# Raw weight copies in the free buffers of the row sums and of the queries

## The chip, the cores and the metric

The kernel runs on one core of one Trainium2 chip. The metric is the device time of one execution in microseconds (us), given as the median of several runs. The core has five engines that work side by side, each through its own list in a fixed order: TensorE (PE) multiplies, VectorE (DVE) and ScalarE (ACT) work element by element, GpSimd (POOL) issues some transfers here, and SyncE (SP) issues most transfers from memory. An instruction that waits holds up everything behind it on its engine.

## What is computed

Two layers of a decoder trunk over 512 positions of width 1024. Each layer has three stages: a gated feed-forward block (`ffn1`), token mixing (`mix`), and a second feed-forward block (`ffn2`). Each stage begins with a norm whose shift, scale and gate are computed from a vector `c`.

```python
def swiglu(x, w_in, w_out):
    gate, up = jnp.split(x @ w_in, 2, axis=-1)
    return (jax.nn.silu(gate) * up) @ w_out
...
    for l in range(DEPTH):
        mod = (c_act @ w_ada[l] + b_ada[l]).reshape(B, N_MOD, D_MODEL)
        sh1, sc1, gt1, sh2, sc2, gt2, sh3, sc3, gt3 = [mod[:, i, None, :] for i in range(N_MOD)]
        hn = rms_norm(h, g_ffn1[l]) * (1.0 + sc1) + sh1
        h = h + 0.5 * (1.0 + gt1) * swiglu(hn, w_ffn1_in[l], w_ffn1_out[l])
        hn = rms_norm(h, g_mix[l]) * (1.0 + sc2) + sh2
        proj = hn @ w_mix_in[l]
        ...
        mixed = jnp.concatenate([y_att, y_rwkv, y_conv], axis=-1) @ w_mix_out[l]
        h = h + (1.0 + gt2) * mixed
        hn = rms_norm(h, g_ffn2[l]) * (1.0 + sc3) + sh3
        h = h + 0.5 * (1.0 + gt3) * swiglu(hn, w_ffn2_in[l], w_ffn2_out[l])
```

The inner width of the feed-forward blocks is 2816, that is 22 tiles of 128. The mixing joins sliding-window attention, a recurrent head group and a short convolution.

## The kernel before

The state `h` lies in memory on the chip as 8 tiles of 128 features by 512 positions. Weights come as tiles of up to 128 x 1024 (512 KB). Each product is made of three matmuls in a reduced format: a number is cast to its high part (`wH`, on ACT, line 101), the rest is its low part (`wL`, on DVE, line 102), and high x high, high x low and low x high are added up (`mm3`, lines 90 to 92). So a weight tile passes four steps: a transfer into a raw buffer `wraw` (`load_w`, line 267), the cast on ACT, the low half on DVE, and the matmuls. There are two `wraw` buffers and four of each half; a transfer waits until the low half of the tile before has read the buffer.

**A feed-forward stage** makes the gated activations in pairs of tiles. Most pairs go through `pair_in`, a scheme of seven products on halves of the matrices; it needs four sums and differences of the normed rows, P1, P2, T3 and T4, which lie in eight buffers with the tag `com` (a high and a low half of each, 4 KB a partition). In the last pair P1 is read in the first product, P2 and T3 later, T4 in the last product of all; after that the `com` buffers are free until the stage ends. Then the output: the 22 activation tiles are taken in two groups; for the second group, output tiles 0 to 5 (`pt`, loop over `i`) are made over all 512 positions, each followed on DVE by its residual (`residual`, line 309, `h <- ps_mm, cg, h`) and on ACT by a square for the next norm (`sq`, line 210), added to `ss` on DVE (line 206). Beside them run the columns that compute the next shifts, scales and gates (`wada`, line 163 on DVE, transfers by POOL).

**The end of a stage** is `close`, with tiles 6 and 7 in halves of 256 positions. PE runs the low half of tile 6, the low half of tile 7, then the high half of tile 6. After five steps of this it runs `stats` (`ps_ss`, line 229): small matmuls over `ss` and the squares of the two residual halves, then `rstd`, `spread` and `apply`, which make the normed rows `hnH`, `hnL` of the next stage while PE finishes tiles 6 and 7. In `close` DVE and ACT keep the order of the text. The halves of tile 7's weights have places of their own (`sum1`, `sum0`, `third`, `first`). The first four weight tiles of the next stage are loaded by the last element of `steps`, `ahead(k)`: 0 and 1 before `close` is called, 2 and 3 inside it. Outside of `close` a scheduler orders the instructions of each engine from the program order, dependencies and estimated costs; the last stage has no successor and its `ahead` does nothing.

**At the end of `mix`** the attention outputs stand in `qr` (the buffer of the queries, 8 KB a partition) until they are split to `y0` to `y3`. Weights of the output tiles come from `wmo1` and, for the last rows, `wmo2`; tiles 6 and 7 have 512 KB transfers. Beside this the recurrent part is finishing, with PE's products `ps_s` waiting for a copy `y` on ACT (line 951).

Of the kernel before, what the change touches and what calls it, by code (L numbers as in the profile page):

```python
# [8 lines left out]
F32 = mybir.dt.float32  # L9
F32R = mybir.dt.float32r  # L10
# [6 lines left out]
P = 128  # L17
# [3 lines left out]
KD = D // P  # L21
# [36 lines left out]
def trunk_kernel(ctx, tc, ins, out, layers=L, phases=("ffn1", "mix", "ffn2")):  # L58
# [24 lines left out]
    def psmm(tags=("mm",)):  # L83
        turn[0] += 1
        return psum([P, T], "ps_mm", tags[turn[0] % len(tags)])

    def mm3(acc, w, k, x, sl, start, stop):

        wH, wL, xH, xL = w[0][:, k], w[1][:, k], x[0][:, sl], x[1][:, sl]
        mm(acc, wH, xH, start=start, stop=False)  # L90
        mm(acc, wH, xL, start=False, stop=False)  # L91
        mm(acc, wL, xH, start=False, stop=stop)  # L92

    def mm6(acc, w, k, x, start, stop):

        for n, (a, b) in enumerate(((0, 0), (0, 1), (1, 0))):
            for sl in HALVES:
                mm(acc[:, sl], w[a][:, k], x[b][:, sl], start=start and n == 0 and sl is HALVES[0], stop=stop and n == 2, skip_group_check=True)  # L98

    def split(hi, lo, src):  # L100
        nc.scalar.copy(hi, src)  # L101
        nc.vector.tensor_sub(lo, src, hi.bitcast(F32))  # L102
# [15 lines left out]
    for i in range(KD):  # L118
        t = hp_.tile([P, T], F32, name=f"h{i}")
# [15 lines left out]
    for name, v in (("eps", EPS), ("eps64", 64 * EPS), ("gneps", GN_EPS), ("nhb", -HB)):  # L135
        t = const.tile([P, 1], F32, name=f"v_{name}")
# [53 lines left out]
    def ada_until(pool, crep, l, i):  # L190
        while todo and todo[0] <= (l, i, KD - 1):
            ada_steps(pool, crep, 1)


    def new_ss():
        return sp.tile([P, T], F32, name="ss", tag="ss")
# [66 lines left out]
    def load_w(src, n=KD, raw=None, pair=None):  # L263

        w = raw or wp.tile([P, KD, P], F32, name="wraw", tag="wraw", bufs=2)
        wH, wL = pair or (wp.tile([P, KD, P], F32R, name=x, tag=x, bufs=4) for x in ("wH", "wL"))
        loads.append(nc.sync.dma_start(w[:, :n], src))
        split(wH[:, :n], wL[:, :n], w[:, :n])
        return wH, wL
# [38 lines left out]
    def residual(pt, i, gate, ss, sl=ALL):  # L308
        done = stt(h[i][:, sl], pt, gate[:, i : i + 1], h[i][:, sl], ALU.mult, ALU.add)  # L309
        add_ss(ss, i, sl)  # L310
        return done

    def last_residual(pt, i, gate, ss, sl):

        residual(pt, i, gate, None, sl)
        return None if ss is None else square(i, sl)

    HAND = {mybir.EngineType.DVE, mybir.EngineType.Activation}

    def close(tiles, gate, ss, steps):  # L320

        stats, spread, apply, low, ahead = steps
        lo_, hi_ = HALVES

        def run(pt, seq, sl, first, at=()):
            for n, (w, k, x) in enumerate(seq):
                mm3(pt, w, k, x, sl, first and n == 0, n == len(seq) - 1)
                for m, f in at:
                    if m == n:
                        f()  # L330

        def half(i, pt, sl):
            return last_residual(pt, i, gate, ss, sl)

        def bank():
            return psmm(BANKS[1:3])[:, : T // 2]

        with tc.manual_schedule(engines=HAND):
            sqs = []
            for i, pt, rest, seq in tiles:  # L340
                first = pt is None
                pt = bank() if first else pt[:, : T // 2]
                run(pt, rest, lo_, first)
                sqs.append(half(i, pt, lo_))
            (i, _, _, seq), (i2, _, _, seq2) = tiles
            pt, late = bank(), []
            run(pt, seq, hi_, True, ((4, lambda: stats(lo_, sqs)), (7, lambda: spread(lo_))))
            ahead(2)
            apply(lo_, range(2))
            late.append(half(i, pt, hi_))  # L350
            apply(lo_, range(2, 4))
            pt = bank()
            run(pt, seq2, hi_, True)
            late.append(half(i2, pt, hi_))
            apply(lo_, range(4, 6))
            stats(hi_, late)
            apply(lo_, range(6, KD))
            spread(hi_)
            apply(hi_, range(4))
            ahead(3)  # L360
            apply(hi_, range(4, KD))
            return low()

    def ffn(l, w_in, w_pair, w_out, hn, im, ss, need, then, ready, first=None):
# [6 lines left out]
        with tc.tile_pool(name="act", bufs=1) as ap_:  # L371
            com = {n: tuple(ap_.tile([P, 4, H2], F32R, name=x, tag="com", bufs=8) for x in ("comH", "comL")) for n in ("P1", "P2", "T3", "T4")}
            ap_.tile([P, (512 - GAP) // 4], F32, name="gap", tag="gap")
            n_first = 2 if first is None else 4
            tiles = (t for t in projector([w_in[l, j, g] for j in range(2 * n_first) for g in range(2)], hn, BANKS[:3], first, 1, ready) if t is not None)
            xs, waiting, done, after = {}, [], [None], [None]
# [117 lines left out]
            def pieces(i, j0, j1, spare=False):  # L494
                n = (j1 - j0) // 2
                for k0 in (j0, j0 + n):
                    turn_[0] += spare
                    w = ap_.tile([P, KD, P], F32, name="wraw", tag="sum0", bufs=1) if spare and turn_[0] % 3 == 0 else None
                    yield k0, n, load_w(w_out[l, i, :, k0 : k0 + n], n, w)
# [5 lines left out]
            for g, (j0, j1) in enumerate(GROUPS):  # L505
# [26 lines left out]
                if g == 0:  # L532
                    cg = small_.tile([P, KD], F32, name="cg", tag="cg")
# [3 lines left out]
                for i in range(KD - 2 * g):  # L537
# [3 lines left out]
                    if g == 0:  # L541

                        k0, k1 = k1, KD if not todo or todo[0] > (l, im + 2, KD) else todo[0][2]
                        if k1 > k0:
                            ts(cg[:, k0:k1], mod[l, im + 2][:, k0:k1], -0.5, -0.5, ALU.mult, ALU.add)
                    pt = psmm(BANKS[:3])
# [2 lines left out]
                            mm3(pt, w, k, xs[k0_ + k], ALL, k0_ + k == j0, k0_ + k == j1 - 1)  # L549
                    done[0] = residual(pt, i, cg, ss if g else None)  # L550
            n = (j1 - j0) // 2
            seqs = [[(w, k, xs[k0 + k]) for k0, n_, w in list(pieces(KD - 2, j0, j1, True)) for k in range(n_)], []]
            for m, tags in enumerate((("sum1", "sum0"), ("third", "first"))):
                pair = tuple(ap_.tile([P, KD, P], F32R, name=x, tag=t, bufs=1) for x, t in zip(("wH", "wL"), tags))
                w = load_w(w_out[l, KD - 1, :, j0 + m * n : j0 + (m + 1) * n], n, None, pair)
                seqs[1] += [(w, k, xs[j0 + m * n + k]) for k in range(n)]
            ada_until(ap_, crep, *need)
            steps = then()
            for m in range(2):
                steps[-1](m)  # L560
            return close([(KD - 2 + m, None, seq, seq) for m, seq in enumerate(seqs)], cg, ss, steps)


    def mix(l, hn, ss, mp, then, ready):
# [5 lines left out]
        def pair(name):  # L570
            return rows_of(name != "y4", (name + "H", name + "L"))
# [32 lines left out]
        cm = small_.tile([P, KD], F32, name="cm", tag="cg")  # L604
# [4 lines left out]
        got = {}  # L609
# [483 lines left out]
        for q in range(2):  # L1093
            x = pair("yr")
            split(*x, yr[q])
            xr.append(x)
        steps = then()
        for n in range(2):
            w = load_w(wo2[l, n], 6)
            for d in range(3):  # L1100
                i = 3 * n + d
                pt = psmm(BANKS[1:3])
                for k in range(2):
                    mm6(pt, w, 2 * d + k, xr[k], k == 0, k == 1)
                residual(pt, i, cm, ss)
            steps[-1](n)
        xs = got["xs"] + xr
        seq = lambda w, ks: [(w, k, xs[k]) for k in ks]
        return close([(i, pt, seq(w, (6, 7)), seq(w, (4, 0, 1, 2, 3, 5, 6, 7))) for i, w, pt in got["last"]], cm, ss, steps)


    what = {"ffn1": ("g1", 0), "mix": ("gm", 3), "ffn2": ("g2", 6)}
    seq = [(l, p) for l in range(layers) for p in phases]

    def normed(n, ss):
        l, p = seq[n]
        g, im = what[p]
        return norm(l, g, im, im + 1, ss)
# [117 lines left out]
    with tc.tile_pool(name="first", bufs=1) as fp:  # L1236
        hn, first = begin(fp)
    ready = None
    for n, (l, p) in enumerate(seq):
        im = what[p][1]  # L1240
        nss = new_ss() if n + 1 < len(seq) else None
        nxt, ws = [], []

        def then():
            if nss is None:
                return [lambda *_: None] * 5
            nhn, scale, *steps = normed(n + 1, nss)
            nxt.append(nhn)
            scale()
            l2, p2 = seq[n + 1]  # L1250
            if p2 == "mix":
                srcs = [ins["wmi"][l2, k] for k in range(4)]
            else:
                srcs = [ins["w1i" if p2 == "ffn1" else "w2i"][l2, *divmod(k, 2)] for k in range(4)]
            return steps + [lambda k: ws.append(load_w(srcs[k]))]

        if p == "mix":
            with tc.tile_pool(name="mix", bufs=1) as mp:
                marks = mix(l, hn, nss, mp, then, ready)
        else:  # L1260
            w, need = ("w1", (l, 7)) if p == "ffn1" else ("w2", (l + 1, 1))
            marks = ffn(l, ins[w + "i"], ins[w + "p"], ins[w + "o"], hn, im, nss, need, then, ready, first)
        first = None
        hn, ready = (nxt[0], (ws, marks)) if nxt else (None, None)
# [85 lines left out]
```

## Time and profile before

| what | value |
|---|---|
| median of 3 runs | 1927.6 us (1924.51 to 1929.95) |
| the profiled execution | 1933.48 us, span 1931.1 us |
| mean granted clock of PE | 0.993 |
| busy: PE, DVE, ACT, POOL | 98%, 73%, 44%, 7% of the span |
| moved by transfers | 308.46 MB, mean 160 GB/s |

A line of the timeline has the start in us, the duration, the engine, the source line, the operation, result and operands, the shape, and in brackets the idle time before it with what ended it. A line of the stretches has the stretch, its length, the busy time of PE, PE's weight loads, DVE, ACT and POOL (with the number of instructions), then the granted clock of PE, the busy share of the transfer engines, and GB/s. A line of the waits has who waited and for what, the total in us, how often, and the longest. The profiled execution is one run with the profiler on, so its time is compared with its own rows, and only differences are carried over to the median.

### The profile page before, as it was taken

Reading aid. Unit: us, or ns where it says so; the run is one execution under the profiler, and the core shown is the slowest. Engines: PE = TensorE matmul, PEld = TensorE weight load, DVE = VectorE, ACT = ScalarE, POOL = GpSimd, SP = SyncE. Lnnn points to the kernel's source line nnn. Section 1 sums busy time; section 2 is a strip of 40 time slices with the busy share of each in tenths; the row PEclk is TensorE's granted clock in tenths of the full one; section 3 lists DMA queues with packets and bytes.
Section 4 is the critical chain, followed back from the end, with each engine's and each line's share of the span. In section 5 each row is a group of like instructions: output and inputs, shape, how many; then the busy total and the mean of one; then the engine's idle time right before and its main releaser. Section 6 shows DMA issues by size and latency. Waiting matters only on the chain. (4 is left out here: it accounts for less than half of the span.)

```text
span 1931.1 us, 37043 instructions
## 1 busy us (share of the span) xinstructions
PE 1887.2 (98%) x15504; PEld 1748.1 (91%) x15504; DVE 1401.1 (73%) x2181; ACT 838.7 (43%) x1264; POOL 130.8 (7%) x212
## 2 busy tenths in 40 slices
PE   8999999999999999999999999999999999999999
PEld 7998899897889999899899988989878899998998
DVE  6687687758976777677878767786598667773862
ACT  4443255346322554155345514534562234532551
POOL 0101100100000000110100021010000000110000
PEclk8999999999999999999999999999999999999999
DMA  7767875621312476886647687662321215764742
GB/s 297 250 162 228 256 197 171 213 77 45 79 39 83 121 197 174 282 211 173 227 127 193 168 274 218 183 224 95 92 61 49 70 51 167 192 216 133 186 124 86
DMA packets 104326, 308.46 MB, mean 160 GB/s; under 512 B 23392, under 2 KB 24416, under 8 KB 103136
## 3 DMA queue, kind: packets, MB, share of 16 engines
q1 hardware_dynamic: 75936, 203.33, 32.2%
q0 software_dynamic: 28224, 102.77, 21.3%
q8 instruction: 121, 1.98, 0.4%
q14 instruction: 45, 0.37, 0.1%
HBM read 302.66 MB, written 3.41 MB: 158 GB/s over the span
## 5 line engine op out<-in xcount | busy, mean ns | idle before, releaser
L101 ACT CAST wH<-wraw 128x1024 fp32r<-128x1024 f32 (+2 forms) x292 | 268.8, 922 | 533.2 <-PE ps_mm L91 176.3
L102 DVE TENSOR_TENSOR wL<-wraw,wH 128x1024 fp32r<-128x1024 f32 (+2 forms) x292 | 308.8, 1059 | 126.4 <-ACT wH L101 125.0
L90 PE MATMUL ps_mm<-actH,wH 128*128 128x512 f32 (+1 forms) x784 | 289.1, 369 | 0.0
L92 PE MATMUL ps_mm<-actH,wL 128*128 128x512 f32 (+1 forms) x784 | 288.7, 368 | 0.0
L91 PE MATMUL ps_mm<-actL,wH 128*128 128x512 f32 (+1 forms) x784 | 288.6, 368 | 0.0
L441 PE MATMUL ps_d<-comH,wH 128*128 128x256 f32 x816 | 228.3, 280 | 4.5 <-ACT s L463 3.9
L442 PE MATMUL ps_d<-comL,wH 128*128 128x256 f32 x816 | 226.9, 278 | 0.0
L443 PE MATMUL ps_d<-comH,wL 128*128 128x256 f32 x816 | 226.9, 278 | 0.0
L98 PE MATMUL ps_mm<-hnH,wH 128*128 128x256 f32 x1040 | 214.7, 287 | 5.0 <-ACT hnH L101 2.9
L98 PE MATMUL ps_mm<-hnL,wH 128*128 128x256 f32 x1040 | 212.5, 283 | 0.0
L98 PE MATMUL ps_mm<-hnH,wL 128*128 128x256 f32 x1040 | 209.9, 282 | 0.5 <-DVE wL L102 0.5
L163 DVE SCALAR_TENSOR_TENSOR wada<-wada,crep 128x1024 f32<-128x1024 f32 x140 | 167.7, 1220 | 47.3 <-DMA wada<-in_wadaT 46.9
L102 DVE TENSOR_TENSOR wL<-sum,wH 128x1024 fp32r<-128x1024 f32 x102 | 124.9, 1225 | 71.1 <-ACT wH L101 70.8
L98 PEld LDWEIGHTS ps_mm<-hnH,wH 128*128 128x128 f32 x1040 | 160.3, 190 | 16.0 <-issue 8.2
L101 ACT CAST wH<-sum 128x1024 fp32r<-128x1024 f32 x102 | 107.5, 1054 | 149.3 <-PE ps_d L442 70.0
L92 PEld LDWEIGHTS ps_mm<-actH,wL 128*128 128x128 f32 x784 | 148.3, 189 | 24.5 <-DVE wL L102 0.3
L91 PEld LDWEIGHTS ps_mm<-actL,wH 128*128 128x128 f32 x784 | 148.3, 189 | 24.4
L90 PEld LDWEIGHTS ps_mm<-actH,wH 128*128 128x128 f32 x784 | 148.4, 189 | 24.2
L98 PEld LDWEIGHTS ps_mm<-hnL,wH 128*128 128x128 f32 x1040 | 160.9, 190 | 6.7 <-issue 5.7
L98 PEld LDWEIGHTS ps_mm<-hnH,wL 128*128 128x128 f32 x1040 | 160.4, 191 | 4.0 <-issue 2.9
L441 PEld LDWEIGHTS ps_d<-comH,wH 128*128 128x128 f32 x816 | 154.7, 190 | 7.1 <-ACT s L463 5.1
L442 PEld LDWEIGHTS ps_d<-comL,wH 128*128 128x128 f32 x816 | 154.6, 190 | 0.0
(402 smaller groups left out, 4240.9 us busy)
## 6 DMA issues: line engine op xcount, KB each, us to landing
wada<-in_wadaT POOLq DMA_DIRECT2D x128, 512.0 KB, 4.8
wraw<-in_wmi SPq DMA_DIRECT2D x40, 512.0 KB
wraw<-in_w2p SPq DMA_DIRECT2D x36, 512.0 KB
wraw<-in_w1p SPq DMA_DIRECT2D x32, 512.0 KB
wraw<-in_w1o SPq DMA_DIRECT2D x32, 384.0 KB
wraw<-in_w2o SPq DMA_DIRECT2D x32, 384.0 KB
wraw<-in_w1i SPq DMA_DIRECT2D x20, 512.0 KB
wraw<-in_w1o SPq DMA_DIRECT2D x32, 320.0 KB
```

Source lines behind the costliest of these rows:

```text
L90: mm(acc, wH, xH, start=start, stop=False)
L91: mm(acc, wH, xL, start=False, stop=False)
L92: mm(acc, wL, xH, start=False, stop=stop)
L98: mm(acc[:, sl], w[a][:, k], x[b][:, sl], start=start and n == 0 and sl is HALVES[0], stop=stop and n == 2, skip_group_check=True)
L101: nc.scalar.copy(hi, src)
L102: nc.vector.tensor_sub(lo, src, hi.bitcast(F32))
L163: stt(w, w, 1.0, crep, ALU.mult, ALU.mult, accum_out=out_)
L441: mm(pt[:, i], wH, x[k][0], start=start and i + k == 0, stop=False, skip_group_check=True)
L442: mm(pt[:, i], wH, x[k][1], start=False, stop=False, skip_group_check=True)
L443: mm(pt[:, i], wL, x[k][0], start=False, stop=k == 3, skip_group_check=True)
```

## The change

The raw copies get other places. In a feed-forward stage eight raw tiles take the tag `com`: two for output tile 6, two for tile 7, and four for the next stage's first weights. In `mix` the next stage's first two raw tiles take the buffer of the queries; the other two stay in `wraw`.

```diff
@@ close
-    def close(tiles, gate, ss, steps):
+    def close(tiles, gate, ss, steps, raws):
...
-            ahead(2)
+            ahead(2, raws[0])
...
-            ahead(3)
+            ahead(3, raws[1])
@@ ffn, after the output tiles 0 to 5
-            seqs = [[(w, k, xs[k0 + k]) for k0, n_, w in list(pieces(KD - 2, j0, j1, True)) for k in range(n_)], []]
-            for m, tags in enumerate((("sum1", "sum0"), ("third", "first"))):
-                pair = tuple(ap_.tile([P, KD, P], F32R, name=x, tag=t, bufs=1) for x, t in zip(("wH", "wL"), tags))
-                w = load_w(w_out[l, KD - 1, :, j0 + m * n : j0 + (m + 1) * n], n, None, pair)
-                seqs[1] += [(w, k, xs[j0 + m * n + k]) for k in range(n)]
+            raws = [ap_.tile([P, KD, P], F32, name="wraw", tag="com", bufs=8) for _ in range(8)]
+            seqs, own = [], (("sum1", "sum0"), ("third", "first"))
+            for i in (KD - 2, KD - 1):
+                seq = []
+                for m in range(2):
+                    pair = None if i < KD - 1 else tuple(ap_.tile([P, KD, P], F32R, name=x, tag=t, bufs=1) for x, t in zip(("wH", "wL"), own[m]))
+                    k0 = j0 + m * n
+                    w = load_w(w_out[l, i, :, k0 : k0 + n], n, raws.pop(0), pair)
+                    seq += [(w, k, xs[k0 + k]) for k in range(n)]
+                seqs.append(seq)
...
             for m in range(2):
-                steps[-1](m)
+                steps[-1](m, raws.pop(0))
@@ mix
         steps = then()
+        raws = mp.tile([P, 2, KD, P], F32, name="wraw", tag="qr")
...
-            steps[-1](n)
+            steps[-1](n, raws[:, n])
@@ then
-            return steps + [lambda k: ws.append(load_w(srcs[k]))]
+            return steps + [lambda k, raw: ws.append(load_w(srcs[k], KD, raw))]
```

PE's and POOL's lists keep their order. DVE's list at the end of the first feed-forward stage (640 columns: a half of an output tile's weights, 1024: a weight tile of the next stage; h_96, h_98 and h_100 are the residuals of tiles 5, 6 and 7), before:

```order
L309 SCALAR_TENSOR_TENSOR h_96<-ps_mm,cg,h_96 128x512
L102 TENSOR_TENSOR wL<-wraw,wH 128x640
L206 TENSOR_TENSOR ss<-ss,sq 128x512
L102 TENSOR_TENSOR wL<-wraw,wH 128x1024
L309 SCALAR_TENSOR_TENSOR h_98<-ps_mm,cg,h_98 128x256
L102 TENSOR_TENSOR wL<-wraw,wH 128x1024
L309 SCALAR_TENSOR_TENSOR h_100<-ps_mm,cg,h_100 128x256
L232 RECIPROCAL rstd<-rstd 128x2
```

The same place on DVE with the change:

```order
L102 TENSOR_TENSOR wL<-wraw,wH 128x1024
L309 SCALAR_TENSOR_TENSOR h_96<-ps_mm,cg,h_96 128x512
L102 TENSOR_TENSOR wL<-wraw,wH 128x1024
L206 TENSOR_TENSOR ss<-ss,sq 128x512
L220 SCALAR_TENSOR_TENSOR gmod<-mod_7_3657,par 128x8
L309 SCALAR_TENSOR_TENSOR h_98<-ps_mm,cg,h_98 128x256
L309 SCALAR_TENSOR_TENSOR h_100<-ps_mm,cg,h_100 128x256
L232 RECIPROCAL rstd<-rstd 128x2
```

Both 1024-column halves now stand ahead of the residual of tile 6, and the residuals of tiles 6 and 7 follow each other.

SP's list at the same stage's end with the change (3820 to 3823 are the raw tiles of output tiles 6 and 7, 3824 to 3827 those of the next stage; the others belong to output tiles 1 and 2):

```order
L267 DMA wraw_3822<-in_w1o 128x640
L267 DMA wraw_3823<-in_w1o 128x640
L267 DMA wraw_3548<-in_w1o 128x640
L267 DMA wraw_3569<-in_w1o 128x640
L267 DMA wraw_3824<-in_wmi 128x1024
L267 DMA wraw_3825<-in_wmi 128x1024
L267 DMA wraw_3605<-in_w1o 128x640
L267 DMA wraw_3626<-in_w1o 128x640
L267 DMA wraw_3826<-in_wmi 128x1024
L267 DMA wraw_3827<-in_wmi 128x1024
```

Before, all sixteen rows from `in_w1o` stood ahead of the first from `in_wmi`; now the loads into `com` stand between those of the output tiles, two by two as the products free their places.

SP's list at the end of the first `mix` (6934 and 6941 are the weights of output tiles 6 and 7), before and with the change:

```order
L267 DMA wraw_6879<-in_wmo1 128x768
L267 DMA wraw_6934<-in_wmo1 128x1024
L267 DMA wraw_6941<-in_wmo1 128x1024
L267 DMA wraw_7011<-in_wmo2 128x768
L267 DMA wraw_7066<-in_w2i 128x1024
```

```order
L267 DMA wraw_6879<-in_wmo1 128x768
L267 DMA wraw_7011<-in_w2i 128x1024 x2
L267 DMA wraw_6934<-in_wmo1 128x1024
L267 DMA wraw_6941<-in_wmo1 128x1024
L267 DMA wraw_7012<-in_wmo2 128x768
```

The next stage's first two loads moved from behind the `wmo1` rows to ahead of 6934. DVE and ACT keep their order at this place.

More of the change, by code (lines that the diff above doesn't have):

```diff
@@ L559, in ffn @@
             for m in range(2):
-                steps[-1](m)
-            return close([(KD - 2 + m, None, seq, seq) for m, seq in enumerate(seqs)], cg, ss, steps)
+                steps[-1](m, raws.pop(0))
+            return close([(KD - 2 + m, None, seq, seq) for m, seq in enumerate(seqs)], cg, ss, steps, raws)
     def mix(l, hn, ss, mp, then, ready):
@@ L1105, in mix @@
                 residual(pt, i, cm, ss)
-            steps[-1](n)
+            steps[-1](n, raws[:, n])
         xs = got["xs"] + xr
         seq = lambda w, ks: [(w, k, xs[k]) for k in ks]
-        return close([(i, pt, seq(w, (6, 7)), seq(w, (4, 0, 1, 2, 3, 5, 6, 7))) for i, w, pt in got["last"]], cm, ss, steps)
+        return close([(i, pt, seq(w, (6, 7)), seq(w, (4, 0, 1, 2, 3, 5, 6, 7))) for i, w, pt in got["last"]], cm, ss, steps, (None, None))
     what = {"ffn1": ("g1", 0), "mix": ("gm", 3), "ffn2": ("g2", 6)}
```

## The prediction

> **What bounds the kernel now.** I read the page first: the busy shares, then the engine TensorE (PE) alone through its waits, then two-microsecond stretches of the span, and last the instructions in time order around the stretches with a hole.
>
> ```profile
> span 1931.1 us, 37043 instructions
> PE 1887.2 (98%) x15504; PEld 1748.1 (91%) x15504; DVE 1401.1 (73%) x2181; ACT 838.7 (43%) x1264; POOL 130.8 (7%) x212
> PE ps_ss L229 <- ACT sq L210: 4.6, 3, 1.8
> PE ps_s L956 <- ACT y L951: 3.7, 2, 2.5
> ```
>
> The page's second line and two lines of PE's waits. PE is busy for 98% of the span, so 1931.1 - 1887.2 = 43.9 us is all that can be won while it does the same work, and the change leaves PE's own list of instructions as it was. The longest wait in total is `ps_ss <- sq`: 4.6 us, three times, the longest 1.8. It stands in `close`, once after each feed-forward stage that has a successor. Three stretches show them:
>
> ```profile
> core 0: us, PE busy (x) PEld busy (x) DVE busy (x) ACT busy (x) POOL busy (x), PEclk, DMA share, GB/s
> 374.00:376.00 2.00, 0.57 (x6) 0.48 (x5) 1.62 (x2) 0.25 (x2) 0.00 (x0) 1.00 0.38 152
> 376.00:378.00 2.00, 1.63 (x14) 1.64 (x15) 0.17 (x1) 0.80 (x3) 0.00 (x0) 1.00 0.78 199
> 972.00:974.00 2.00, 0.97 (x11) 0.89 (x9) 1.18 (x2) 0.42 (x1) 0.00 (x0) 1.00 0.22 72
> 1320.00:1322.00 2.00, 0.70 (x8) 0.61 (x6) 1.62 (x2) 0.26 (x1) 0.00 (x0) 1.00 0.55 207
> 1322.00:1324.00 2.00, 1.52 (x13) 1.53 (x14) 0.08 (x1) 0.79 (x3) 0.00 (x0) 1.00 0.65 188
> 1324.00:1326.00 2.00, 2.00 (x13) 2.00 (x13) 1.23 (x3) 0.82 (x1) 0.00 (x0) 0.61 0.19 78
> 1326.00:1328.00 2.00, 2.00 (x12) 2.00 (x12) 1.81 (x6) 0.91 (x2) 0.00 (x0) 0.53 0.39 106
> 1328.00:1330.00 2.00, 2.00 (x20) 2.00 (x19) 1.50 (x4) 1.35 (x3) 0.00 (x0) 1.00 0.40 156
> ```
>
> PE lacks 1.43 + 0.37 = 1.8 us at 374 to 378, 1.03 at 972 and 1.30 + 0.48 = 1.78 at 1320. The two rows after that last hole show something more: the granted clock is 0.61 and 0.53, and 25 matmuls pass in 4 us where the next row has 20 in 2. Why PE waits is seen on the engines ahead of it (VectorE is DVE, ScalarE is ACT), in time order:
>
> ```profile
> 367.79 0.73 ACT L101 CAST wH<-wraw 128x640 fp32r<-128x640 f32 x1 [3.48 <-DMA wraw<-in_w1o]
> 373.10 1.05 ACT L101 CAST wH<-wraw 128x1024 fp32r<-128x1024 f32 x1 [0.41 <-DMA wraw<-in_wmi]
> 374.18 1.23 DVE L102 TENSOR_TENSOR wL<-wraw,wH 128x1024 fp32r<-128x1024 f32 x1 [1.94 <-ACT wH L101]
> 375.32 0.48 DVE L309 SCALAR_TENSOR_TENSOR h<-ps_mm,cg,h 128x256 f32<-128x256 f32 x1
> 375.90 0.42 ACT L210 ACTIVATE sq<-h 128x256 f32<-128x256 f32 x1 [1.75 <-DVE h L309]
> ...
> 372.27 0.28 PE L90 MATMUL ps_mm<-actH,wH 128*128 128x256 f32 x1
> ...
> 374.07 0.28 PE L229 MATMUL ps_ss<-ones_r,ss 128*128 128x1 f32 x2
> ...
> 376.37 0.38 PE L229 MATMUL ps_ss<-ones_r,sq 128*128 128x1 f32 x2 [1.80 <-ACT sq L210]
> ```
>
> The residual of output tile 7 (375.32) had its sum ready at about 372.3, when PE began the next run. It stands in DVE's row behind the low half of the next stage's second weight tile, which waits for ACT's cast, which waits for a transfer into one of two `wraw` buffers. The chain is transfer, cast, low half, residual, square, statistic: a transfer ends last.
>
> **The change part by part.** *1. The loads at the end of a feed-forward stage.* The four transfers of tiles 6 and 7 (320 KB each) and four of the next stage (512 KB each) are free of the two `wraw` buffers; their places come free with the products P1, P2, T3 and T4 of the last pair. On DVE the next weights now stand ahead of tile 5's residual, so the residuals of tiles 6 and 7 follow each other. I follow the first stage. The last gating column of this stage ends on DVE at 364.05:
>
> ```profile
> 362.90 1.23 DVE L163 SCALAR_TENSOR_TENSOR wada<-wada,crep 128x1024 f32<-128x1024 f32 x1
> 369.29 0.69 DVE L206 TENSOR_TENSOR ss<-ss,sq 128x512 f32<-128x512 f32 x1
> 365.68 0.74 DVE L309 SCALAR_TENSOR_TENSOR h<-ps_mm,cg,h 128x512 f32<-128x512 f32 x1
> ```
>
> Behind it come three low halves of 640 columns, two of 1024, tile 5's residual and its addition to `ss`, and tile 6's residual. With the pitches of these rows that is 3 x 0.8 + 2 x 1.2 + 0.7 + 0.7 + 0.4 = 6.6 us: DVE is free for tile 7 at about 370.6, and PE ends that half at 372.3. So tile 7's residual runs 372.4 to 372.9 and its square to 373.4, before PE reaches the statistic at 374.07. There is 0.7 us in hand on this path and 1.7 on DVE. The term is -(1.8 + 1.0 + 1.8) = -4.6 us; its ends are 0, if all three statistics are as late as before, and -4.6, since a wait cannot fall below zero. I take -4.6, since the chain clears it. After the statistic nothing moves against PE: `rstd`, `ahead(2)` and the norm stand in the same row as before.
>
> *2. The half clock.* Besides the one at 1324 there are three more such stretches, all after holes that the change leaves:
>
> ```profile
> 690.00:692.00 2.00, 2.00 (x11) 2.00 (x11) 0.00 (x0) 0.00 (x0) 0.00 (x0) 0.50 1.01 328
> 1538.00:1540.00 2.00, 0.85 (x8) 0.66 (x6) 0.61 (x1) 1.05 (x1) 0.00 (x0) 1.00 0.10 40
> 1540.00:1542.00 2.00, 0.59 (x6) 0.53 (x7) 1.93 (x4) 1.02 (x3) 0.00 (x0) 1.00 0.29 33
> 1544.00:1546.00 2.00, 2.00 (x12) 1.88 (x10) 0.28 (x1) 0.00 (x0) 0.00 (x0) 0.50 0.67 197
> 1640.00:1642.00 2.00, 2.00 (x12) 2.00 (x11) 0.00 (x0) 0.00 (x0) 0.00 (x0) 0.53 0.97 383
> ```
>
> One costs 4 us less the 2.7 that 25 matmuls need at 37 to 38 in 4 us: 1.3 us. Of the three removed holes one was followed by it, so I take -1.3; the ends are 0 and two of them, -2.6, as both 1.8 us holes are alike.
>
> The Trainium skill ("TensorE: Matmul & The Clock Gate", Part 1, "What's actually happening") says that the clock halves after an idle window of about 3.4 us of a free-running counter and asks for no idle gap longer than that. By this rule a hole of 1.8 us would halve nothing, and the sum would be -4.6 alone. The trace differs: 1.8 us of idle at 1320 was followed by 4 us at 0.57. The same page's free-running window would explain why the equal hole at 374 was not.
>
> *3. Early transfers beside the last pair and the output tiles.* SP issues in order, so tiles 1, 2 and 3 of the output weights now stand behind transfers that wait for PE. DMA has room there, and little later:
>
> ```profile
> 304.00:308.00 4.00, 4.00 (x37) 4.00 (x37) 4.00 (x5) 2.18 (x4) 0.00 (x0) 1.00 0.29 112
> ...
> 320.00:324.00 4.00, 4.00 (x38) 4.00 (x37) 2.58 (x4) 1.50 (x3) 0.00 (x0) 1.00 0.37 109
> 324.00:328.00 4.00, 4.00 (x21) 3.36 (x20) 3.49 (x5) 3.25 (x6) 0.00 (x0) 1.00 0.41 103
> 340.00:360.00 20.00, 20.00 (x90) 16.57 (x89) 17.52 (x32) 5.98 (x9) 4.22 (x8) 1.00 0.92 303
> 318.91 0.73 ACT L101 CAST wH<-wraw 128x640 fp32r<-128x640 f32 x1 [1.19 <-PE ps_d L442]
> ...
> 327.97 0.71 ACT L101 CAST wH<-wraw 128x640 fp32r<-128x640 f32 x1
> ```
>
> T3's product ends near 319 (it released the cast at 318.91), T4's near 325, where PE changes to the output tiles (21 matmuls in 4 us for 38). Behind the two 512 KB transfers that T3 frees, 1 MB at the 303 GB/s of the third row is 3.5 us, so tile 2's weights land by about 325, ahead of their cast at 327.97. I cost this at 0. Its cover is that cast's lead over PE: at 90 matmuls in 20 us a tile of 30 takes 6.7 us, so tile 2 is multiplied from about 338. In the busy stretch 340 to 360 there is now less to move.
>
> *4. The end of the mixing stage.* Two 512 KB loads into the queries' buffer stand on SP ahead of the weights of output tiles 6 and 7 and start when the last query is split, at 575.3.
>
> ```profile
> 574.63 0.68 DVE L102 TENSOR_TENSOR y3L<-qr,y3H 128x512 fp32r<-128x512 f32 x1
> 576.00:580.00 4.00, 4.00 (x71) 3.70 (x70) 1.62 (x2) 1.43 (x2) 0.00 (x0) 1.00 0.00 0
> 583.31 1.78 ACT L101 CAST wH<-wraw 128x1024 fp32r<-128x1024 f32 x2 [4.65 <-DMA wraw<-in_wmo]
> 596.44 1.05 ACT L101 CAST wH<-wraw 128x1024 fp32r<-128x1024 f32 x1 [3.10 <-PE ps_mm L98]
> ```
>
> They fall into 576 to 580, when DMA is idle. 1 MB takes 3.5 us, until about 579.7, which is when tile 6's load can start (its buffer is read out then). The gain is nothing, since the cast they serve (596.44) waits for PE. The price is 0; its ends are 0 and +1 us in each of two layers, were half of one transfer still in the way. I take 0 by the row that shows no traffic.
>
> *5. The last stage* has no successor. There ACT and DVE each get one split of tile 7 ahead of `up` in the last pair.
>
> ```profile
> 1866.64 0.69 DVE L478 TENSOR_TENSOR up<-ps_d,up 128x512 f32<-128x512 f32 x1 [1.25 <-PE ps_d L443]
> ```
>
> With 0.7 us more on ACT and 0.8 on DVE `up` moves to at most 1868.1, and PE needs its bank only after another product of 24 matmuls, 2.6 us, at about 1869.1. I take 0, with ends 0 and +0.5. The four small constants of `mix` move to a later place on DVE, of 0.1 us each in rows that PE does not wait for: 0.
>
> **Sum.** -4.6 - 1.3 = -5.9 us. Against the profiled execution's 1933.48 us this gives 1927.6. That execution lies 5.9 us above the median of three runs, 1927.6, to which I apply the same difference: 1921.7 us.
>
> **The rivals.**
> (a) The holes close and the clock gains nothing, because in most executions no half-clock stretch followed them, or because another hole catches it: 1927.6 - 4.6 = 1923.0. For it: the hole at 374 had none. Against: the one at 1320 had.
> (b) Something is late next. If the gating columns end 3 us later than 364, DVE reaches tile 7 at 373.6 and a good half of each hole stays: about 1925. For it: DMA at 0.92 of its time at 340 to 360. Against: the change takes traffic out of that stretch.
> (c) Slower: at the mixing end tile 6's weights come late behind the two early loads, and cast, low half, tile 7's load and the `ps_s` wait (2.5 us already at 1538) all shift. It decides from 3 us in each of the two layers, which cancels 5.9; at 4 us it gives about 1930. For it: the casts there already wait 4.65 us for such a load. Against: the idle row at 576.
> (d) The statistic is as late as before, for a reason other than DVE's row: 1927.6. Against: DVE's order itself changes there.
>
> **How the numbers follow.** Forecast 0.52, (a) 0.20, (b) 0.13, (c) 0.08, (d) 0.07. About 0.3%, 5.8 us, is what a measurement of this kernel tells from no change, so the line lies at 1921.8, on the forecast itself. The forecast's own range is 1919 to 1924, as none to two half-clock stretches are saved; six tenths of it (0.31) lie beyond the line, and I add half of (a) for runs in which the old kernel met more of them: faster 0.41, slower 0.08 from (c), same the rest, 0.51. The range runs from 1917, where the two stretches and a spread of the runs (1924.51 at the lowest, 3 us below the median) come together, to 1927.5, which takes in (a), (b) and half of (d).
>
> **What would show it.** Right: PE's waits have no `ps_ss <- sq` over 0.3 us; the two half-tile residuals (L309, 128x256) no longer have a 1024-column low half between them; no half clock after the three places; the first transfers of `in_wmi` start before 330. The `ps_s <- y` wait stays at 2 to 4 us in total: if it has grown to 7, (c) is true. Wrong: new waits of PE for `wH` or `wL` among the output tiles, or `ps_d` waiting for `up` in the last pair.

## The result, and the profile after

| | before | changed | ratio, 95% interval |
|---|---|---|---|
| median, first comparison | 1928.57 us (10 runs) | 1921.68 us (10 runs) | 0.9963 [0.9951, 0.9976] |
| median, the changed kernel run again | 1929.63 us (20 runs) | 1919.63 us (5 runs) | 0.9945 [0.9932, 0.9958] |
| profiled execution | 1933.48 us, span 1931.1 | 1922.28 us, span 1920.5 | |

The changed kernel is faster by 6.9 us in the first comparison and by 10.0 us in the second. The forecast was 5.9 us. Both intervals lie below 1. Two of the first lines of the page after:

```profile
span 1920.5 us, 37038 instructions
PE 1884.7 (98%) x15504; PEld 1747.4 (91%) x15504; DVE 1400.5 (73%) x2181; ACT 838.1 (44%) x1264; POOL 130.9 (7%) x212
```

The four longest of PE's waits (who waited for what, total us, times, longest):

```profile
PE ps_g L443 <- DVE wL L102: 4.5, 3, 2.6
PE ps_d L441 <- ACT s L463: 3.6, 2, 1.8
PE ps_s L961 <- ACT y L956: 3.1, 2, 2.0
PE ps_mm L98 <- ACT hnH L101: 2.9, 1, 2.9
```

`ps_ss <- sq`, 4.6 us and first in the list before, is no longer in it. Lines 956 and 961 are 951 and 956 of before; the change added five lines above them. The three places now lie at 370, 962 and 1310. The stretches there, columns as before (PE, PEld, DVE, ACT, POOL busy with counts, then the granted clock, the transfers' share and GB/s):

```profile
370.00:372.00 2.00, 2.00 (x19) 2.00 (x18) 0.64 (x2) 0.84 (x2) 0.00 (x0) 1.00 0.00 0
372.00:374.00 2.00, 2.00 (x20) 2.00 (x19) 0.05 (x1) 0.35 (x2) 0.00 (x0) 1.00 0.00 0
...
964.00:966.00 2.00, 2.00 (x19) 2.00 (x18) 0.48 (x1) 0.42 (x1) 0.00 (x0) 1.00 0.00 0
...
1312.00:1314.00 2.00, 2.00 (x20) 2.00 (x18) 0.48 (x1) 0.42 (x1) 0.00 (x0) 1.00 0.04 8
1314.00:1316.00 2.00, 2.00 (x19) 2.00 (x19) 0.17 (x1) 0.71 (x2) 0.00 (x0) 1.00 0.00 0
```

PE is busy in all of each, at full clock, and almost nothing is transferred: the weights had come earlier, their transfers issued on SP from 317 on (two rows of SP in time order, the duration being that of issuing):

```profile
316.99 0.80 SPq L267 DMA_DIRECT2D wraw<-in_wmi  x2
...
322.43 0.80 SPq L267 DMA_DIRECT2D wraw<-in_wmi  x2
```

DVE and ACT in time order at the first place:

```profile
367.87 1.21 DVE L102 TENSOR_TENSOR wL<-wraw,wH 128x1024 fp32r<-128x1024 f32 x1
369.00 0.68 DVE L206 TENSOR_TENSOR ss<-ss,sq 128x512 f32<-128x512 f32 x1
...
369.68 0.48 DVE L309 SCALAR_TENSOR_TENSOR h<-ps_mm,cg,h 128x256 f32<-128x256 f32 x1
370.56 0.48 DVE L309 SCALAR_TENSOR_TENSOR h<-ps_mm,cg,h 128x256 f32<-128x256 f32 x1 [0.40 <-PE ps_mm L92]
...
371.14 0.42 ACT L210 ACTIVATE sq<-h 128x256 f32<-128x256 f32 x1 [0.53 <-DVE h L309]
373.65 0.26 ACT L231 ACTIVATE rstd<-ps_ss,v_eps 128x2 f32<-128x2 f32 x1 [2.09 <-PE ps_ss L229]
```

The 1024-column low half runs without a wait. Tile 7's residual (370.56) waits for PE alone, and ACT then waits 2.09 us for PE's statistic; before, PE waited 1.8 us for ACT.

**Where the 10.6 us between the two spans lie.** I added up over one-microsecond stretches, from 40 us to 22 us before the end, what PE was not busy ("idle") and what it lost to the clock (one less the granted clock, times its busy time). Idle fell from 32.9 to 24.3 us, clock loss rose from 6.6 to 8.1, and the same two losses in the first 40 us fell from 13.0 to 10.9. That is 9.2 of the 10.6; the rest I could not place. Not all of it belongs to the change. The 2.1 us of the first 40 us lie ahead of every place that the change touches, and two holes elsewhere differ too. Before had 3.2 us of idle at 1172 to 1182, which after lacks, and after has a new one:

```profile
1026.00:1028.00 2.00, 0.86 (x8) 0.66 (x6) 2.00 (x3) 1.43 (x2) 0.87 (x1) 1.00 0.50 203
1028.00:1030.00 2.00, 0.54 (x2) 0.54 (x3) 2.00 (x3) 2.00 (x4) 0.00 (x0) 0.86 0.85 129
1030.00:1032.00 2.00, 2.00 (x12) 2.00 (x11) 1.68 (x2) 0.05 (x1) 0.00 (x0) 0.50 1.03 272
```

These rows are the hole (2.6 us) and half clock behind it. Its start is on ACT, 18 us earlier:

```profile
1008.79 1.05 ACT L101 CAST wH<-sum 128x1024 fp32r<-128x1024 f32 x1 [4.94 <-DMA sum<-in_w1p]
```

The cast of the first weight sum waited 4.94 us for its transfer, 2.84 before, and I take it that ACT, DVE and then PE came 2 us later by it. Whether that is the change's doing was the first question for the runs.

### The profile page after: what moved, and what is told of

Its sections match the earlier page's. It is cut to its first block, busy times and chain, and to the rows that moved or that the text cites. A ratio compares the mean times of both kernels' runs of the same rounds, so it can differ in the third digit from the quotient of the medians.

```text
span 1920.5 us, 37038 instructions
## 1 busy us (share of the span) xinstructions
PE 1884.7 (98%) x15504; PEld 1747.4 (91%) x15504; DVE 1400.5 (73%) x2181; ACT 838.1 (44%) x1264; POOL 130.9 (7%) x212
```

## The experiments

Each kernel was timed in the same session as the kernel before. Ratios are to that kernel, with 95% intervals.

**1. The changed kernel again.** No edit.

> The changed kernel once more, for a second profile. If the holes that stood only in one of the two first profiles (before: 3.2 us at 1172 to 1182; after: 2.6 us at 1026 to 1030 with 4 us of half clock behind it) come from transfers whose time differs from run to run, then this profile shows no ps_ss wait again, but the 1026 hole is smaller than 1 us or a hole of 1 to 3 us stands at another pair stage. If they are effects of the change, the 1026 hole is there again with 2 us or more and the 1172 place is without one. Time by either: 1918 to 1925 us, 0.995 to 0.998 of the kernel before.

Measured 1919.63 us, ratio 0.9945 [0.9932, 0.9958], no `ps_ss` wait. The hole at 1026 had 1.0 us and 1.3 us stood at 1170: the first case. In eleven of the thirteen profiles the size of that hole goes with the wait of the one cast, whatever part of the change a kernel has: waits of 4.3 to 4.9 us stand with holes of 2.6 to 2.7, waits of 3.2 to 4.1 with 1.4 to 1.5, and waits under 2.9 with 1.0 or less. Two profiles of runs that follow below do not fit: fill has a wait of 4.4 and a hole of 1.8, s1_before a wait of 2.8 and a hole of 1.6. Rows of mix_only (feed-forward ends as before; hole 2.7 us) and of ffn_only (hole 1.0 us):

```profile
1018.23 1.05 ACT L101 CAST wH<-sum 128x1024 fp32r<-128x1024 f32 x1 [4.68 <-DMA sum<-in_w1p]
```

```profile
1008.56 1.05 ACT L101 CAST wH<-sum 128x1024 fp32r<-128x1024 f32 x1 [2.84 <-DMA sum<-in_w1p]
```

The same kernel had the hole at 2.6 us in one execution and at 1.0 in another, and mix_only, with the old feed-forward ends, has it at 2.7. So the hole is not the price of the change. That the longer transfer makes it fits most of the profiles; the two that do not fit leave this open.

**2. Only the feed-forward part, and 3. only the mixing part.**

```diff
 ffn_only
-        raws = mp.tile([P, 2, KD, P], F32, name="wraw", tag="qr")
-            steps[-1](n, raws[:, n])
+            steps[-1](n, None)
 mix_only: ffn as before, and
-            return close([...], cg, ss, steps, raws)
+            return close([...], cg, ss, steps, (None, None))
```

> Only the feed-forward part of the change; at the mixing end all raw copies lie in wraw as before. Theory (the row of DVE at the three feed-forward ends carries the gain, the mixing part is worth 0): no ps_ss wait over 0.3 us, 1920 to 1924 us, ratio 0.9955 to 0.9975. Rival (the mixing part carries a part of the gain, by earlier transfers at 572 to 580 and 1515 to 1522): 1925 us or more, ratio over 0.998, and the holes at 676 to 690 and 1620 to 1640 or at 586 to 600 are larger than in the changed kernel by 1 us or more.

> Only the mixing part of the change; the feed-forward ends are as before. Theory: the three ps_ss waits stand as before (4.6 us in total, 1.0 to 1.8 each), 1927 to 1930 us, ratio 0.999 to 1.001. Rival (mixing part gains): 1925 us or less, ratio under 0.998. Rival (mixing end late behind the early loads): the waits ps_s on y grow by 1 us or more, 1930 us or more.

ffn_only: 1919.70 us, 0.9951 [0.9937, 0.9964]. mix_only: 1930.55 us, 1.0001 [0.9990, 1.0012]. Within these intervals all of the gain is in the feed-forward ends. In mix_only the wait that the change is about is there again, and larger than in the first profile; five stretches at 374 show what it drew (the wait first):

```profile
PE ps_ss L229 <- ACT sq L210: 6.6, 3, 2.7
```

```profile
374.00:376.00 2.00, 0.17 (x2) 0.17 (x2) 1.27 (x2) 0.42 (x1) 0.00 (x0) 1.00 0.25 64
376.00:378.00 2.00, 2.00 (x12) 2.00 (x13) 0.17 (x1) 0.64 (x2) 0.00 (x0) 0.59 0.63 242
378.00:380.00 2.00, 2.00 (x12) 2.00 (x11) 1.22 (x1) 0.55 (x1) 0.00 (x0) 0.50 0.03 8
380.00:382.00 2.00, 2.00 (x12) 2.00 (x11) 1.53 (x4) 0.91 (x2) 0.00 (x0) 0.50 0.59 143
382.00:384.00 2.00, 2.00 (x14) 2.00 (x14) 1.79 (x5) 1.35 (x3) 0.00 (x0) 0.71 0.30 119
```

Here the first place, which had no half clock in the profile before, has some 7 us of it.

**4. Only the order, and 5. only the place.** The diff changes two things at once: where the raw copies lie, and the order in which DVE meets the low halves and the residuals. order_only keeps all copies in `wraw` and moves one low half behind the statistic (and the one after it a little further back); place_only keeps the new places and puts a low half back between the two residuals.

```diff
 order_only (from the kernel before; only at feed-forward ends)
-            for m in range(2):
-                steps[-1](m)
-            return close([...], cg, ss, steps)
+            steps[-1](0)
+            return close([...], cg, ss, steps, True)
... close, where the new argument is called more
-            ahead(2)
+            ahead(1 if more else 2)
             apply(lo_, range(2))
             late.append(half(i, pt, hi_))
+            if more:
+                ahead(2)
 place_only (from the changed kernel; its two calls of ahead before close are gone)
                 run(pt, rest, lo_, first)
+                if len(raws) == 4:
+                    ahead(len(sqs), raws[len(sqs)])
                 sqs.append(half(i, pt, lo_))
+            raws = raws[-2:]
```

> The kernel before with all raw copies in wraw, but at a feed-forward end the next stage's second weight tile is made after the first statistic instead of ahead of it, so DVE makes the residuals of tiles 6 and 7 one after the other. Theory (the order on DVE is the cause, the place of the raw copies only its means): no ps_ss wait over 0.3 us, gain 4 to 6 us: 1922 to 1925 us, ratio 0.9970 to 0.9985. Rival (the early transfers are what pays: DVE would still stand behind a low half that waits for a transfer): ps_ss waits of 1 us or more stay, or new waits of the same sum behind them, 1927 us or more, ratio over 0.999.

> The changed kernel, but at a feed-forward end DVE makes the low half of the next stage's second weight tile between the residuals of tiles 6 and 7, as in the kernel before. Theory (the residual was late because the low half ahead of it waited for a transfer; with the raw copy there early the low half takes only its 1.2 us, and DVE is still free before PE ends tile 7): no ps_ss wait over 0.3 us, the same time as the changed kernel, 1919 to 1923 us, ratio 0.994 to 0.997. Rival (the order on DVE alone decides): ps_ss waits of 1 to 2 us in the three places, 1924 to 1929 us, ratio 0.998 or more.

order_only: 1923.39 us, 0.9969 [0.9954, 0.9984]. place_only: 1921.79 us, 0.9960 [0.9946, 0.9974]. In both the `ps_ss <- sq` wait is gone, so neither the old order nor the old place is enough by itself to make PE wait; either remedy takes away the chain. DVE's rows at the first place, order_only:

```profile
370.20 1.23 DVE L102 TENSOR_TENSOR wL<-wraw,wH 128x1024 fp32r<-128x1024 f32 x1 [0.56 <-ACT wH L101]
371.34 0.87 DVE L309 SCALAR_TENSOR_TENSOR h<-ps_mm,cg,h 128x256 f32<-128x256 f32 x2
```

and place_only:

```profile
371.34 1.22 DVE L102 TENSOR_TENSOR wL<-wraw,wH 128x1024 fp32r<-128x1024 f32 x1 [1.42 <-ACT wH L101]
372.48 0.48 DVE L309 SCALAR_TENSOR_TENSOR h<-ps_mm,cg,h 128x256 f32<-128x256 f32 x1
```

In order_only one low half is out of the row, and the two residuals (one row, x2) follow each other at 371.34. In place_only the low half still stands ahead of tile 7's residual and still waits 1.42 us for its cast, but it starts early enough. place_only also shows a price that did not appear in the two profiles of the changed kernel: a wait of PE for `wL` of an output tile of the second feed-forward stage, 1.6 us at 945. PE's waits of this kind, and then the cast on ACT behind which that one lies:

```profile
PE ps_mm L92 <- DVE wL L102: 2.2, 2, 1.6
```

```profile
943.23 0.72 ACT L101 CAST wH<-wraw 128x640 fp32r<-128x640 f32 x1 [6.22 <-DMA wraw<-in_w2o]
```

**6. and 7. Which of the raw copies.**

```diff
 both (from the changed kernel; the mixing part as in ffn_only)
-            raws = [... for _ in range(8)]
+            raws = [... for _ in range(4)]
 tiles67
-                steps[-1](m, raws.pop(0))
-            return close([...], cg, ss, steps, raws)
+                steps[-1](m, None)
+            return close([...], cg, ss, steps, (None, None))
 next_only: tiles 6 and 7 are loaded by the lines of the kernel before
```

> Only the raw copies of output tiles 6 and 7 lie in com; the next stage's four stay in wraw, and the mixing part is undone. DVE's row at the feed-forward end is that of the changed kernel. Theory (enough that tiles 6 and 7 leave the two wraw buffers: the next stage's transfers then find them free some 5 us earlier): no ps_ss wait over 0.3 us, 1919 to 1924 us, ratio 0.994 to 0.9975. Rival (the next stage's raw copies must be early, since DVE stands behind their low halves): ps_ss waits of 0.5 us or more in at least two places, ratio 0.998 or more.

> Only the next stage's four raw copies lie in com; those of output tiles 6 and 7 stay in wraw, and the mixing part is undone. Theory (either half of the raw copies is enough, as the low halves of the next stage no longer wait): no ps_ss wait over 0.3 us, ratio 0.994 to 0.9975. Rival (tile 7's own weights, four transfers through two wraw buffers, are then what is late): a wait for wH or wL of 0.5 us or more in the last two output tiles or ps_ss waits that stay, ratio 0.998 or more.

tiles67: 1920.26 us, 0.9958 [0.9943, 0.9973]. next_only: 1919.39 us, 0.9951 [0.9934, 0.9968]. Neither has a `ps_ss <- sq` wait; either half of the copies is enough. Of what the rival for next_only named, one wait of 0.4 us for a low half of an output tile is there. At the first place tile 7's residual in tiles67 waits for PE and not the other way round:

```profile
371.05 0.48 DVE L309 SCALAR_TENSOR_TENSOR h<-ps_mm,cg,h 128x256 f32<-128x256 f32 x1 [2.48 <-PE ps_mm L92]
```

**8. PE kept at work in the holes.** The kernel before, with eight matmuls ahead of the first statistic; they add work, and nothing reads their result.

```diff
+            def first_stats():
+                if fill:
+                    pw = psum([P, 4, P], "ps_fill", "mm")
+                    for _ in range(fill):
+                        mm(pw, ones_r, wide, start=True, stop=True)
+                stats(lo_, sqs)
... first_stats stands in the place of stats; fill is 8 at feed-forward ends
```

> The kernel before with eight idle-time matmuls of 512 columns (a bank that nobody reads) on PE ahead of the first statistic of each feed-forward end, so that PE works where it waited. The residual of tile 7 stays as late. Theory (the half clock at these places follows PE's own idle time): ps_ss waits under 0.5 us, no half clock within 6 us behind the three places, and the time falls by what the half clock cost, 1 to 3 us, less the 0.5 to 1 us by which the matmuls outlast the shortest hole: 1926 to 1929 us, ratio 0.998 to 1.000. Rival (the half clock has nothing to do with these holes, and comes from the load of the whole stretch): one or two of the three places have half clock behind them all the same, ratio 1.000 to 1.001.

1930.88 us, 1.0002 [0.9989, 1.0015]. One `ps_ss` wait of 1.4 us was left, and behind none of the three places was there half clock (PE in time order at the first place; then the group of all added matmuls with its busy time in us and the mean in ns; then two stretches):

```profile
372.96 2.00 PE L353 MATMUL ps_fill<-ones_r 128*128 128x512 f32 x8
376.72 0.38 PE L229 MATMUL ps_ss<-ones_r,sq 128*128 128x1 f32 x2 [1.42 <-ACT sq L210]
```

```profile
L353 PE MATMUL ps_fill<-ones_r 128*128 128x512 f32 x32 | 8.0, 392 | 0.0
```

```profile
376.00:378.00 2.00, 1.28 (x11) 1.28 (x12) 0.16 (x1) 0.54 (x2) 0.00 (x0) 1.00 0.54 164
378.00:380.00 2.00, 2.00 (x20) 2.00 (x19) 1.06 (x2) 1.07 (x2) 0.00 (x0) 1.00 0.27 107
```

The clock followed the theory at the three places. One profile says little by itself: in the kernels with the old ends half of such places have no half clock behind them (step 2 below), so none in three would come up once in eight by chance. But the mean granted clock is on record for every timed run, and it was 0.9948 over the 12 runs of this kernel and 0.9919 over the 20 of the kernel before beside it: about 5.6 us less lost to the clock, as an estimate (0.0029 of 1930 us).

The time, expected at 1926 to 1929 us, did not fall. The expectation left out that the last stage ends in `close` too. The eight matmuls ran there as well, at 1916.7, where PE had no wait to fill, so 32 of them added 8.0 us and not 6. They replaced 3.6 us of waits (1.4 left of a mean of 5.0) and, at the price found in step 2 below, 3.0 us of clock: 1.4 us more than before. Measured were 1.7 us more (1930.88 against 1929.16), with an interval from 2.1 less to 2.9 more. So the time fits the price of the half clock and does not prove it. The ratio lies where the rival put it (1.000 to 1.001), but the rival's sign, half clock behind one or two of the places, is not there.

**9. The kernel before again.**

> The kernel before once more, for a second profile. Theory (the sizes of the three holes and which of them draws the half clock differ from run to run): three ps_ss waits again, in total 4 to 7 us, half clock behind zero to three of the places. The 3.2 us at 1172 is smaller or elsewhere if it is a matter of transfers in one run, and there again with 2.5 us or more if the kernel's order sets it.

1927.72 us in one run. `ps_ss` waits of 4.0 us in total, the longest 2.9 (at the first place, where the first profile had 1.8), half clock behind that one only. The idle at 1172 was 2.1 us: smaller, but there.

**10. and 11. The next wait of the same kind.** In the first pair of the seven products of the second feed-forward stage ACT casts a weight sum, which waits for DVE, ahead of the copy `s` for which PE waits. The edit makes ACT copy first, in every such pair; s1_first has it on the changed kernel, s1_before on the kernel before.

```diff
-                nc.scalar.copy(s1, pD)
+                s1_done = nc.scalar.copy(s1, pD)
...
-                prod(pF, hl(S), B22, False)
+                with tc.issue_after(s1_done.ins):
+                    S4 = hl(S)
+                prod(pF, S4, B22, False)
```

> The changed kernel, and in every pair of the seven products ACT makes the copy s of the first sum (which PE waits for) ahead of the cast of the third weight sum (which waits for DVE). Theory: the wait ps_d on s, 1.8 us at 680 and at 1622 in both kernels, falls to under 0.3, with the half clock behind it (1.5 us each) in at least one of the two: 4 to 6.5 us less than the changed kernel, 1914 to 1917 us, ratio to the kernel before 0.991 to 0.9935. Rival (PE only meets the next late low half there, and the clock stays): 1919 to 1921 us, ratio 0.9945 to 0.996, with ps_g on wL or ps_d on wH grown by 1 us or more at those places.

> The kernel before with only the other edit: ACT makes the copy s of the first sum ahead of the cast of the third weight sum. Theory (the two gains are separate places and add up): ps_ss waits as before, the ps_d wait on s of 3.6 us falls under 1.5 us in total, and the time is 8 to 10 us below the kernel before, that is the changed kernel with both edits less the changed kernel: 1919 to 1922 us, ratio 0.9945 to 0.9965. Rival (a part of the gain was the three feed-forward ends starting earlier): ratio 0.997 to 0.999.

s1_first: 1911.71 us, 0.9918 [0.9900, 0.9935], which beats both kernels. s1_before: 1923.20 us, 0.9978 [0.9965, 0.9992]. Rows of ACT of the changed kernel at 1625, and a stretch behind them:

```profile
1625.82 1.04 ACT L101 CAST wH<-sum 128x1024 fp32r<-128x1024 f32 x1 [1.32 <-DVE sum L474]
1626.77 0.58 ACT L463 COPY s<-ps_d 128x512 f32<-128x512 f32 x1
```

```profile
1628.00:1630.00 2.00, 2.00 (x11) 2.00 (x11) 0.12 (x1) 0.00 (x0) 0.00 (x0) 0.50 1.01 299
```

and of s1_first at the same place, with the stretch behind it:

```profile
1615.30 0.58 ACT L463 COPY s<-ps_d 128x512 f32<-128x512 f32 x1
1616.67 1.06 ACT L101 CAST wH<-sum 128x1024 fp32r<-128x1024 f32 x1 [0.79 <-DVE sum L474]
```

```profile
1616.00:1618.00 2.00, 2.00 (x18) 2.00 (x19) 2.00 (x3) 1.06 (x1) 0.00 (x0) 1.00 0.74 131
```

The cast lost nothing, since it waits for DVE anyway. s1_first has no half clock at all between 40 us and 22 us before its end. That alone would prove little, as next_only, without this edit, has none either in its profile. Over all profiles it is clearer: in the eleven without the edit half clock follows 17 of the 22 places like this one (two in each execution, near 680 and near 1620, with 2.6 to 2.8 us of idle time each), in the two with it none of the four. Of the wait `ps_d <- s`, 3.6 us before, 1.9 us were left in s1_first, of which 1.4 are on the next copy of the same kind (line 468). The ratio of s1_first is in the expected range, its time is 2 us below it. The expectation for s1_before, 8 to 10 us, was too large: 4.6 us were measured. The savings of the two edits alone, 0.22% and 0.37 to 0.55%, add up to 0.59 to 0.77%; together they measured 0.82%, with an interval from 0.65 to 1.00. So they are compatible with adding up, and the runs do not show more than that.

## Why the prediction was right, and where its sizes were off

**Step 1, the feed-forward ends: right.** Forecast -4.6. All three `ps_ss <- sq` waits vanished in the changed kernel, and in every variant that keeps one of the two remedies. The four profiles with the old ends and without filling (before, before_again, mix_only, s1_before) have waits of 4.6, 4.0, 6.6 and 4.8 us, 5.0 in the mean. The chain was read rightly: take away any one link (the transfer's place, the order on DVE, either half of the copies) and the wait is gone. Of the two margins in the working, one came out. From the end of the square (371.14 + 0.42) to PE's statistic at 372.16 there is 0.6 us, as against 0.7. The other did not: the working had DVE free 1.7 us before PE ends its half, and in the profile after DVE waits only 0.40 us for PE. DVE's row itself took 6.4 us, as against 6.6. But PE came 1.9 us earlier to this place than before, about what the first 40 us of that execution lost less (2.1), while the gating columns, which wait for transfers of their own, ended only 0.3 us earlier. The cover on DVE was thinner than the working says.

**Step 2, the half clock: the right mechanism, the term too small.** Forecast -1.3, from one stretch in three at 1.3 us each. In those four profiles 7 such stretches followed six of the 12 holes (one hole drew two), and each cost 1.7 us by the granted clock (about 3.4 us at 0.5): 3.0 us per execution. The 1.3 came from a rate of another place, 37 to 38 matmuls in 4 us, where the row right behind the stretch has 20 in 2. With 5.0 for the waits that makes 8.0. The seven kernels without the three waits that carry no other gain (the changed kernel twice, ffn_only, order_only, place_only, tiles67, next_only) were faster by 6.9, 10.0, 9.9, 6.2, 7.4, 7.5 and 8.4 us in the medians: 8.0 in the mean. That the two agree to a tenth is luck, since each of the seven has an interval of 2.4 to 3.3 us to either side. Two more records show that the half clock goes with the holes. None stands behind the 24 places of the eight profiles in which the waits are gone. And the mean granted clock was 0.9922 over the 57 runs of the kernel before that were timed beside the variants, and 0.9944 over the 51 runs of the seven kernels: as an estimate, 0.0022 of 1920 us, or 4.2 us less lost to the clock, at these places and all others. One profile gave only one draw of a quantity that differs between executions. The Trainium skill ("TensorE: Matmul & The Clock Gate", Part 1, "What's actually happening") names a free-running window of about 3.4 us. The length of a stretch, about 3.4 us, agrees with it; that the clock halves after a whole idle window does not, as the six holes were of 0.9 to 2.9 us.

**Step 3, early transfers at 0: right in the profiles of the changed kernel,** which have no wait for `wH` or `wL` among the output tiles; the first transfers of `in_wmi` were issued at 317, ahead of the 330 named. place_only, with the same order of transfers, had 1.6 us of one, so the cover is thin.

**Step 4, the mixing end at 0: right.** mix_only alone is 1.0001 [0.9990, 1.0012]. The two early loads did start in the idle stretch, and the casts of `in_wmo` wait 4.62 us as against 4.65 before:

```profile
579.44 1.79 ACT L101 CAST wH<-wraw 128x1024 fp32r<-128x1024 f32 x2 [4.62 <-DMA wraw<-in_wmo]
```

`ps_s <- y` came to 3.1 us, 3.7 before. It never grew to the 7 of rival (c). The working has a slip here on which nothing hung: 575.3 and 3.5 us make 578.8, not 579.7.

**Step 5, the last stage at 0: right.** `up` follows `gate` by 3.29 us as against 2.72, and PE does not wait for it.

**The rivals.** (a), closed holes without a gain by the clock, gave 1923.0. The clock loss behind the three places, 3.0 us in the mean, went to zero in all profiles with the change, which speaks against it; but clock losses at other places differ so much between executions (8.1 us in all in the first profile after, 3.4 in the second) that two profiles alone would not have shown it. (b), (c) and (d) fell: nothing was late next at the ends, the mixing end cost nothing, and the wait went. The size given to (b) does not follow from its rows: with the residual at 373.6 and not 375.32, 1.7 of the 1.8 us of that hole would be gone, and not less than half.

**The forecast and the chances.** That 1921.7 was forecast and 1921.68 measured is luck. The kernel before came out at 1928.57 in that comparison and not at 1927.6, so the gain was 6.9 us where 5.9 were forecast, and over the seven kernels it was 8.0. The chances put a little more on a difference too small to tell (0.51) than on faster (0.41); with the clock term at 3.0 the forecast would have lain beyond the line. Nor are the 43.9 us that PE is not busy all that can be won: the busy time holds the time at half clock, which the same working counts as a gain, and it fell from 1887.2 to 1884.7 us with the same 15504 matmuls.

## What to carry to other kernels

When PE waits for a small result, read the rows of the engine that makes it backwards to the first instruction that itself waits for a transfer: that instruction blocks the result only by its place in the row, and either data that come earlier or a later place for it will do. Look for the same pattern everywhere before stopping: here a copy behind a cast on another engine was worth 0.2 to 0.5% more for one ordering edge. Price a short wait of PE with the clock it may cost behind it, and from several profiles, since one may hold none or two.

## What was not expected of the hardware

Whether a hole is followed by half clock is not fixed by its length. In s1_before 0.9 us of idle at 966 was followed by it; in mix_only 2.3 us at 1323 to 1326 were not (stretches of s1_before, then of mix_only):

```profile
966.00:968.00 2.00, 1.10 (x12) 1.02 (x10) 1.06 (x2) 0.42 (x1) 0.00 (x0) 1.00 0.15 33
...
970.00:972.00 2.00, 2.00 (x11) 2.00 (x10) 2.00 (x3) 0.35 (x1) 0.00 (x0) 0.50 0.00 0
```

```profile
1324.00:1326.00 2.00, 0.00 (x0) 0.00 (x0) 1.53 (x2) 0.37 (x1) 0.00 (x0) 1.00 0.43 172
...
1328.00:1330.00 2.00, 2.00 (x19) 2.00 (x18) 1.53 (x2) 0.44 (x1) 0.00 (x0) 1.00 0.03 12
```

The loss was 1.7 us each time, twice that at 374 in mix_only. What decides between the two cases stays open. The transfer of one weight sum held a cast up for 4.94 us in one execution of the changed kernel and for 2.87 in another, and for 2.5 to 4.9 us over all profiles; the hole of PE behind it had between nothing and 2.7 us.
